# Retention heads 1 to 7 with seven block products for q with k and for value with gate

## The chip, the cores and the metric

The kernel is one program on one core of a Trainium2 chip. The metric is the device time of one execution in microseconds (us). The core's engines run side by side, each through its own queue of instructions in a fixed order: TensorE (PE in the profile, with PEld for its weight loads), VectorE (DVE), ScalarE (ACT), GpSimd (POOL) and SyncE (SP, which here issues DMA transfers). They wait for each other through semaphores.

## The reference, cut to what matters

The model has two layers over 512 latent tokens and 256 context tokens of width 1024, all in float32. Layer 0 is neighbourhood attention beside spatial gating, then a gated FFN with a short convolution. Layer 1 is a retention with eight heads, then an FFN of the same form. The change lies in the retention:

```python
def retention_mixer(h_ctx, h_lat, w_in, log_decay, gn_g, w_out, ctx_out):
    ...
    q, k, v, g = jnp.split(h_lat @ w_in, splits, axis=-1)   # 512 x 1024 times 1024 x 6144
    q = apply_rope(q.reshape(B, T, H, dk), cos, sin)        # H = 8, dk = 128, dv = 256
    k = apply_rope(k.reshape(B, T, H, dk) * dk ** -0.5, cos, sin)
    ...
    for d in range(2):                                      # forward and backward
        s_ctx = retention_final_state(rev(kc), rev(vc), lg)
        outs_lat.append(rev(retention_chunked(rev(q), rev(k), rev(v), lg, s_ctx)))
    # per-head norm of the sum, times silu(g), times w_out (2048 x 1024)
    y_lat = retention_output(outs_lat[0] + outs_lat[1], g, gn_g, w_out)
```

So for each head there are, of the latent tokens, a product for q and for k (1024 x 128 weights each), one for the value and one for the gate (1024 x 256 weights each), then scores, states and outputs of the head, and the head's share of the output projection, summed over heads into `y`.

## The kernel before, in words

**Split products.** A float32 product is made of three PE products in a faster format. `split` makes a high part with ACT (line 211) and the remainder with DVE (line 212); `mm3` then issues three matmuls (lines 256, 257, 258): high by high, high by low, low by high. Weights come from DRAM by SP into a raw buffer (`raw_unit`, three buffers), are split into a slot (`slot`; in the retention six slots `w0` to `w5`), and are named `rwk`, `rwq`, `rwv`, `rwg`, `rwo` here. `h0c` and `h1c` are the high and low parts of the normed tokens, which lie transposed in SBUF, the width along the partitions.

**A head of the retention** (`for h in range(8)`, line 1446): `proj_t` makes k (`rk`) and q (`rq`) of the latent tokens, 8 chunks of the contraction times 3 matmuls, each 128 x 512. `rope` takes them out of PSUM: two half copies by ACT (`swk`, `swq`, line 1259), a product by DVE (`m1k`, `m1q`, line 1260), a product by POOL (line 1261), a sum by DVE (line 1262), and a split. `nat` makes value and gate (`rn`), two token blocks at a time: 48 matmuls of 128 x 256 each for context value, latent value (two) and gate (two). Then scores (`rs`, `sd`), states (`stc`, `stl`), and the outputs within and across chunks (`ro`, `rx`), with the norm. `gated(h-1)` transposes the gated output of the head before (`rt`, then `gt`), and `out_group` multiplies it by two weight tiles: eight pieces `wr` of 128 x 512, six matmuls each, which DVE adds from PSUM to the four `y` tiles in SBUF (line 718; ACT copies for the first head, line 716). The pieces of a head are thus made during the next one; those of heads 6 and 7 are made at the end, in `out_last`. The `e` tiles are the head's decay weights, `acc` belongs to the adaLN products that are made in the background of the retention (`bg`).

**Seven products elsewhere.** Both FFNs already make their input products by blocks: of a 2 x 2 by 2 x 2 block product seven block products of sums are made instead of eight, with the weight sums on DVE, and context and latent outputs of FFN 0 are collected in DRAM by POOL (`yp`, four buffers, lines 1770 to 1774).

**Order.** The order of every engine's instructions is written out: `ORDER` is a packed table which `queue` decodes, and the instructions that the Python code makes are issued in its order. PSUM tiles come from three tags: A with four banks, B and C with two each.

## Time and profile before

| | |
|---|---|
| median of 3 runs | 1777.94 us (1776.95 to 1779.11) |
| profiled execution | 1775.4 us, of which the span of instructions is 1773.6 us |
| mean granted TensorE clock | 0.996 |
| busy: PE, DVE, ACT, POOL | 1747.3, 1394.7, 1025.0, 344.5 us |
| layer 0, attention and FFN | 0 to about 897 us |
| retention, heads 0 to 7 | about 897 to 1396 us |
| end of the retention and FFN 1 | 1396 to 1773.6 us |

The page gives busy time by engine, the span in 40 slices with busy tenths, the chain of work that ended last, the costliest groups of instructions, and the DMA transfers. Busy time of PE counts a matmul from its start to its modelled end, and matmuls overlap; how long one holds the array is read from the distance of starts in the timeline. The transposes `rt` of the head before mark where heads 1 to 7 begin: at about 949, 1015, 1081, 1146, 1212, 1277 and 1343 us.

### The profile page before, as it was taken

The page shows a single profiled execution, that of the slowest core. Times are in us where ns is not written, and L with a number is a line of the kernel's source. Part 1 is how long each engine was busy: PE and PEld are TensorE (multiplying, and loading weights), DVE is VectorE, ACT ScalarE, POOL GpSimd, SP SyncE. Part 2 cuts the span into 40 slices and gives each one's busy share as a digit, 9 for nine tenths or more (in the row PEclk, how much of TensorE's full clock was granted, in tenths as well). Part 3 has the DMA queues.
Part 4 walks back from the last instruction along what each step waited for, and adds up shares of the span by engine and source line. Part 5 has one row for each costly group of instructions (what it writes and reads, how often), then busy time and mean ns, then how long its engine had stood idle before and what let it go on. Part 6 is the DMA issues. An engine that isn't in the chain of part 4 may idle for free.

```text
span 1773.6 us, 28862 instructions
## 1 busy us (share of the span) xinstructions
PE 1747.3 (99%) x11024; PEld 1570.8 (89%) x11024; DVE 1394.7 (79%) x2363; ACT 1025.0 (58%) x1883; POOL 344.5 (19%) x462
## 2 busy tenths in 40 slices
PE   8999999999999999999999999999999999999997
PEld 4898888799999999999898998998999799999996
DVE  4887887898888878889877677666755799998896
ACT  7533667786556565656665434434444577767673
POOL 1102322230132321221311001101101200222212
PEclk9999999999999999999999999999999999999999
DMA  8345331364698877887643342341321335887763
GB/s 310 118 144 157 115 90 43 107 180 139 155 185 182 189 155 161 180 163 162 243 140 122 107 126 83 96 119 61 104 74 49 119 98 177 209 207 188 172 160 125
DMA packets 84398, 253.44 MB, mean 143 GB/s; under 512 B 11026, under 2 KB 11538, under 8 KB 84260
## 3 DMA queue, kind: packets, MB, share of 16 engines
q1 hardware_dynamic: 55044, 191.27, 34.2%
q0 software_dynamic: 26912, 51.95, 17.5%
q10 hardware_dynamic: 2304, 8.39, 1.2%
q8 instruction: 86, 1.41, 0.3%
q14 instruction: 52, 0.43, 0.1%
HBM read 191.80 MB, written 39.85 MB: 131 GB/s over the span
## 4 chain that ended last, share of the span: by engine, by line
PE 47%; DVE 1%; POOL 1%; ACT 1%; issue 0%; DVEq 0%; POOLq 0%; ACTq 0%
PE px L255 5%; PE rn L258 4%; PE rn L256 4%; PE rn L257 4%; PE wf L256 2%; PE wf L257 2%; PE wf L258 2%; PE py L255 2%; PE wr L258 1%; PE wr L257 1%; PE wr L256 1%; PE rk L257 1%; PE rk L256 1%; PE rk L258 1%; PE rq L258 1%; PE rq L257 1%
## 5 line engine op out<-in xcount | busy, mean ns | idle before, releaser
L366 DVE SCALAR_TENSOR_TENSOR acc<-ar,cs,acc 128x512 f32<-128x512 f32 x256 | 191.4, 768 | 7.3 <-DMA ar<-in_adaw 5.0
L255 PE MATMUL px<-hs,wc 128*128 128x384 f32 (+1 forms) x480 | 108.4, 308 | 0.2 <-ACT pre L1614 0.2
L1774 POOL DMA_DIRECT2D yf<-yp x64 | 55.5, 960 | 263.7 <-ACT yp L1770 236.7
L256 PE MATMUL rn<-rwv,h0c 128*128 128x256 f32 x384 | 106.6, 282 | 0.0
L258 PE MATMUL rn<-rwv,h1c 128*128 128x256 f32 x384 | 105.8, 281 | 0.4 <-DVE h1c L212 0.4
L257 PE MATMUL rn<-rwv,h0c 128*128 128x256 f32 x384 | 104.8, 280 | 0.0
L255 PE MATMUL px<-blk,wb 128*128 128x384 f32 (+1 forms) x480 | 103.3, 308 | 0.4 <-ACT pre L1614 0.4
L1770 ACT COPY yp<-wf 128x512 f32<-128x512 f32 x118 | 68.6, 583 | 51.6 <-PE wf L258 47.0
L1627 DVE SCALAR_TENSOR_TENSOR cv<-pre,cw,cv 128x769 f32<-128x769 f32 (+1 forms) x88 | 77.4, 884 | 22.5 <-ACT cv L1626 22.5
L1626 ACT ACTIVATE cv<-pre,cw 128x770 f32<-128x770 f32 (+1 forms) x88 | 80.9, 925 | 24.4 <-DVE pre L1619 22.1
L1614 ACT ACTIVATE pre<-px 128x256 f32<-128x256 f32 (+2 forms) x160 | 55.4, 370 | 54.1 <-PE px L255 32.5
L255 PEld LDWEIGHTS px<-hs,wc 128*128 128x128 f32 x480 | 80.8, 188 | 5.7 <-ACT pre L1614 0.5
L255 PEld LDWEIGHTS px<-blk,wb 128*128 128x128 f32 x480 | 79.2, 188 | 5.1 <-ACT pre L1614 1.0
L1630 DVE SCALAR_TENSOR_TENSOR cv<-pre,cw,cv 128x769 f32<-128x769 f32 (+1 forms) x88 | 77.5, 883 | 0.8
L258 PEld LDWEIGHTS rn<-rwv,h1c 128*128 128x128 f32 x384 | 71.7, 189 | 2.3 <-DVE h1c L212 0.7
L256 PEld LDWEIGHTS rn<-rwv,h0c 128*128 128x128 f32 x384 | 71.9, 188 | 2.1
L257 PEld LDWEIGHTS rn<-rwv,h0c 128*128 128x128 f32 x384 | 71.7, 189 | 1.5
L1774 POOL DMA_DIRECT2D yd<-yp x48 | 45.4, 973 | 135.2 <-ACT yp L1770 123.6
L257 PE MATMUL rn<-rwg,h0c 128*128 128x256 f32 x256 | 70.1, 280 | 0.0
L258 PE MATMUL rn<-rwg,h1c 128*128 128x256 f32 x256 | 69.9, 280 | 0.0
L255 PE MATMUL px<-hs,wd 128*128 128x384 f32 x240 | 69.9, 338 | 0.0
L256 PE MATMUL rn<-rwg,h0c 128*128 128x256 f32 x256 | 69.7, 279 | 0.0
(1546 smaller groups left out, 6398.9 us busy)
## 6 DMA issues: line engine op xcount, KB each, us to landing
ar<-in_adaw SPq DMA_DIRECT2D x96, 512.0 KB, 3.7
yf<-yp POOLq DMA_DIRECT2D x64, 256.0 KB, 4.9
yd<-yp POOLq DMA_DIRECT2D x54, 256.0 KB, 5.1
yd<-ypg POOLq DMA_DIRECT2D x54, 256.0 KB, 5.4
fin<-xd SPq DMA_DIRECT2D x8, 512.0 KB, 10.9
xn<-in_x SPq DMA_DIRECT2D x6, 512.0 KB
xb<-in_x SPq DMA_DIRECT2D x6, 512.0 KB
xd<-xb ACTq DMA_DIRECT2D x6, 512.0 KB, 3.6
```

The lines of the kernel that those rows point to most:

```text
L255: mm = lambda *p, **k: self.T.matmul(*p, skip_group_check=True, **k)
L256: mm(out, lhs[0], rhs[0], start=first, stop=False)
L257: mm(out, lhs[0], rhs[1], start=False, stop=False)
L258: mm(out, lhs[1], rhs[0], start=False, stop=last)
L366: V.scalar_tensor_tensor(out=acc[s], in0=raw[:, kk * 512 : kk * 512 + 512], scalar=self.cs[:, 8 * s + k : 8 * s + k + 1], in1=acc[s], op0= ...
L1614: S.activation(pre[:, i, c : c + w], ps[:, b : b + w], AF.Copy, scale=scale)
L1626: S.activation(d, s, AF.Identity, scale=w1, bias=b)
L1627: V.scalar_tensor_tensor(out=d[:, 1:W], in0=s[:, 0 : W - 1], scalar=w0, in1=d[:, 1:W], op0=ALU.mult, op1=ALU.add)
L1630: V.scalar_tensor_tensor(out=d[:, 0 : W - 1], in0=s[:, 1:W], scalar=w2, in1=d[:, 0 : W - 1], op0=ALU.mult, op1=ALU.add)
L1770: S.copy(v, ps)
L1774: G.dma_start((yd[t] if first else y[t])[:, o], v, accum_op=ALU.add)
```

## The change

For heads 1 to 7 the products of the latent tokens are made by blocks. Tokens (two halves of 256) and contraction (two halves of 512) make a 2 x 2 block matrix, `blk`; k with q, and value with gate, are the other two block columns. Seven products `X`, `Y`, `Z` are accumulated in three PSUM banks and read in between.

- `token_sums`, once at the end of head 0: four sums of the token blocks (`s1` to `s4`; `f` on POOL, then DVE, then splits). `s2` and `s4` lie in the space of the `y` tiles, `s3` over block 21 of the tokens.
- `k_unit`, `q_units`, `vg_units`: weight differences by `less` on POOL, in place in the raw buffers; four of 128 x 512 for q with k, four of 128 x 1024 for value with gate, each head. The results are split like the weights (`rwt1` to `rwt4`; halves of `rwq1` to `rwq3`). The raw weights of k and q and of the value's second half have two buffers of their own (`rawx`).
- `qk_lat`: seven products of 12 matmuls 128 x 256 (`xk`, `yk`, `zk`), summed in SBUF as `ks` and `qs` by ACT copies and DVE sums, on which `rope` then works. `vg_lat`: seven products of 24 matmuls 128 x 256 (`xv`, `yv`, `zv`). The context's value stays with `nat`.
- `out_away`: the pieces `wr` of heads 0 to 5 are copied by ACT into one of two `yp` buffers and sent by POOL to DRAM (`yd`), added there after the first head. In head 7 four loads on SP bring `y` back.
- Weight slots go from six to five.

Counts of instructions, before and after: PE matmuls 10882 and 10966 (1344 `rn` and 336 `rk`/`rq` fewer, 1764 of 128 x 256 more), DVE 2333 and 2400, ACT 1769 and 1915, POOL 467 and 579, SP 402 and 406.

```diff
-            rp = self.phase(ctx, "retp", 3, SLOT)
+            rp = self.phase(ctx, "retp", 2, SLOT)
...
-            order += [... ("w3", SLOT), ("w4", SLOT), ("w5", SLOT)]
+            order += [... ("w3", SLOT), ("w4", SLOT), ("rawx", 1024, 2), ("sx", 2048), ("yp", 512, 2)]
...
+            def less(out, x, y):
+                G.tensor_tensor(out=out, in0=x, in1=y, op=ALU.subtract)
...
+            def q_units(h):
...
+                w[11], w[21] = halves(d["wk"])
+                less(rk[:, H[0]], rq[:, H[0]], rk[:, H[0]])
+                less(rq[:, H[0]], rq[:, H[1]], rq[:, H[0]])
+                w["t", 1], w[22] = halves(self.slot(f"rwq1{h}"))
+                self.split(*w["t", 1], rk[:, H[0]])
+                self.split(*w[22], rq[:, H[1]])
...
+            def qk_lat(h, w):
...
+                qk_product(X, w[11], blk[11], "only")
+                S.copy(ks[:, A], X)
+                qk_product(Z, w[21], blk[12], "only")
+                V.tensor_tensor(out=ks[:, A], in0=ks[:, A], in1=Z, op=ALU.add)
+                qk_product(Y, w["t", 1], blk["s", 1], "only")
+                S.copy(qs[:, B], Y)
+                qk_product(X, w["t", 2], blk["s", 2], "onto")
+                S.copy(qs[:, A], X)
+                qk_product(X, w["t", 3], blk["s", 3], "onto")
+                V.tensor_tensor(out=qs[:, B], in0=qs[:, B], in1=X, op=ALU.add)
+                qk_product(Y, w[22], blk["s", 4], "onto")
+                V.tensor_tensor(out=qs[:, A], in0=qs[:, A], in1=Y, op=ALU.add)
+                qk_product(X, w["t", 4], blk[22], "onto")
+                S.copy(ks[:, B], X)
...
+            def vg_units(h):
...
+                v0, g0 = self.raw_unit(row(0, 0), f"rwv0{h}"), self.raw_unit(row(16, 0), f"rwg0{h}")
+                w[11] = parts(v0, "v0")
...
+                less(v0, g0, v0)
...
+                w["t", 1] = parts(v0, "t1")
+                less(g0, g1, g0)
...
+                w["t", 3] = parts(g0, "t3")
+                w[22] = parts(g1, "g1")
+                less(g1, g1, v0)
...
+            def out_away(f, w, first):
+                for t in toks:
+                    c = self.gcol(t)
+                    for n in range(2):
+                        ps = self.ps(f"wr{t}{n}", "B")
+                        for x, ((gh, gl), (wh, wl)) in enumerate(zip(f, w)):
+                            self.mm3(ps, (gh[:, c], gl[:, c]), (wh[:, H[n]], wl[:, H[n]]), x == 0, x == 1)
+                        z = rp.tile([P, 512], F32, name="ypr", tag="yp", bufs=2)
+                        S.copy(z, ps)
+                        if first:
+                            G.dma_start(yd[t][:, H[n]], z)
+                        else:
+                            G.dma_start(yd[t][:, H[n]], z, accum_op=ALU.add)
...
-                    psk = self.ps(f"rk{h}", "A")
-                    self.proj_t(psk, wk, 0)
-                    k_lat(h, psk)
-                    wq = qk(h, 0, "q")
-                    psq = self.ps(f"rq{h}", "A")
+                    w = q_units(h)
                     decay(h)
                     f = gated(h - 1)
-                    self.proj_t(psq, wq, 0)
-                    q_lat(h, psq)
+                    qk_lat(h, w)
                     self.bg()
                     if h < 7:
-                        self.out_group(f, w_out(h - 1), y, toks, h == 1, None, f"r{h - 1}")
+                        out_away(f, w_out(h - 1), h == 1)
...
+                    for t in toks:
+                        y[t] = self.ytile(t, f"yr{t}")
+                        self.load(y[t], yd[t])
```

The table `ORDER` is replaced as a whole (one line of it stands for all):

```diff
-c-pmlXLRJ)b>@8l3aJ1TfI{V*t4J1E%sDi3X0w}Qv%AR-(|M-jO!tHilQjyXFr#Eiqd2mHNA_wYTN+zFYiVuo`gqqX$79L)*p`pit6ke`uXoQ```CLgs>
+c-oD82ecdKb>{sCGlRi241mF)_woR|-g_^6y^@cQkL9sS6sy=oijpWxlqI>yawJ){<w%x`Y{|AP+p*)mPP}olC7Wz=a*{YcC)rKBn@#MT-JDH1C!1{c-h
...
```

What it moves, at three places in head 4. TensorE before, where q of head 4 ends and the first output piece of head 3 (`wr300`) begins; each row is a matmul, destination, then moving and stationary operand:

```order
L257 MATMUL rq4_11875<-h1c_8692,rwq4_11872 128x512
L258 MATMUL rq4_11875<-h0c_8691,rwq4_11872 128x512
L256 MATMUL rq4_11875<-h0c_8691,rwq4_11872 128x512
L256 MATMUL wr300_11947<-rwo30_11939,gt03_11882 128x512
L257 MATMUL wr300_11947<-rwo30_11939,gt03_11882 128x512
L258 MATMUL wr300_11947<-rwo30_11939,gt13_11883 128x512
L256 MATMUL wr300_11947<-rwo31_11944,gt03_11882 128x512
```

The same place after; the lines 269 to 271 are those of `mm3`, `rwq24` is a split weight difference and `s40r` a token sum:

```order
L269 MATMUL yk4_12132<-s41r_9692,rwq14_12092 128x256
L269 MATMUL xk4_12131<-h1c_8692,rwq24_12099 128x256
L269 MATMUL xk4_12131<-h0c_8691,rwq24_12099 128x256 x2
L269 MATMUL xk4_12131<-h1c_8692,rwq24_12099 128x256
L270 MATMUL wr00_12259<-rwo30_12251,gt03_12113 128x512
L269 MATMUL xk4_12131<-h0c_8691,rwq24_12099 128x256
L271 MATMUL wr00_12259<-rwo30_12251,gt03_12113 128x512
L269 MATMUL xk4_12131<-h0c_8691,rwq24_12099 128x256
```

The 512-wide projection is gone, and matmuls of several products and of the output piece alternate one by one.

GpSimd before, from the norm of head 3 to that of head 4 (`e`: decay weights, `swk` and `swq`: rope):

```order
L1407 TENSOR_TENSOR rrr3_11802<-rrr3_11802,mhalf_107 128x2
L1252 TENSOR_TENSOR e04_11876<-e04_11876,e14_11878 128x384
L1261 TENSOR_TENSOR swk4_11862<-swk4_11862,sin_9093 128x512
L1253 TENSOR_TENSOR e04_11876<-e04_11876,ident_95 128x128
L1261 TENSOR_TENSOR swq4_11925<-swq4_11925,sin_9093 128x512
L357 MEMSET acc180_12235 128x512
```

And after, from the first output piece on (`rwv04r` and so on are the raw weights of head 4):

```order
L1465 DMA yd0r_9101<-ypr_12266 128x512
L1489 TENSOR_TENSOR swk4_12227<-swk4_12227,sin_9095 128x512
L1465 DMA yd0r_9101<-ypr_12276 128x512
L1293 TENSOR_TENSOR rwv04r_12369<-rwg04r_12371,rwv04r_12369 128x1024
L1465 DMA yd1r_9102<-ypr_12286 128x512
L1489 TENSOR_TENSOR swq4_12237<-swq4_12237,sin_9095 128x512
L1465 DMA yd1r_9102<-ypr_12296 128x512
L1293 TENSOR_TENSOR rwg04r_12371<-rwg14r_12408,rwg04r_12371 128x1024
L1465 DMA yd2r_9103<-ypr_12306 128x512
L371 MEMSET acc180_12590 128x512
L1465 DMA yd2r_9103<-ypr_12316 128x512
L1477 TENSOR_TENSOR e04_12107<-e04_12107,e14_12109 128x384
```

Eight DMA issues and eight subtractions have come in between, and the rope's two products stand behind issues of output pieces.

ScalarE after, at the same place (before, it has the `gt` and `swq` of head 4 and the splits of `rwg40` here, and no copy of an output piece, as DVE added those):

```order
L1461 COPY ypr_12266<-wr00_12259 128x512
L1483 ACTIVATE swk4_12227<-ks4_12129 64x512 x2
L1461 COPY ypr_12276<-wr01_12269 128x512
L1483 ACTIVATE swq4_12237<-qs4_12130 64x512 x2
L225 ACTIVATE ah170_12357<-acc170_11622 128x512
L1461 COPY ypr_12286<-wr10_12279 128x512
L225 ACTIVATE rwt14_12437<-rwv04r_12369 128x1024
L225 ACTIVATE rk04_12225<-ks4_12129 128x512
L1461 COPY ypr_12296<-wr11_12289 128x512
L225 ACTIVATE rq04_12235<-qs4_12130 128x512
```

From the third on, each copy needs the buffer of the copy two before it, and the splits of weights and of the rotated k and q stand behind these copies.

More of the change, by code (lines that the diff above doesn't have):

```diff
@@ new lines, in q_units @@
+            def q_units(h):
+                d = hd[h]
+                rk = d["rk"]
+                rq = rawx(a["ret_qk"][h * P : (h + 1) * P], f"rwq{h}")
+                halves = lambda u: [[x[:, c] for x in u] for c in H]
+                w = {}
+                w[11], w[21] = halves(d["wk"])
[4 more added lines that the diff above has]
+                self.split(*w[22], rq[:, H[1]])
+                less(rq[:, H[1]], rq[:, H[1]], rk[:, H[0]])
+                less(rk[:, H[1]], rk[:, H[1]], rq[:, H[1]])
+                w["t", 2], w["t", 3] = halves(self.slot(f"rwq2{h}"))
+                self.split(*w["t", 2], rq[:, H[1]])
+                self.split(*w["t", 3], rq[:, H[0]])
+                w["t", 4] = halves(self.slot(f"rwq3{h}"))[0]
+                self.split(*w["t", 4], rk[:, H[1]])
+                return w
@@ L1423, in gated @@
                 if h == 7:
[L1424 removed]
+                    sx = rp.tile([P, 2, 2, 512], F32R, name="gt7", tag="sx", bufs=1)
+                    gt = [sx[:, i] for i in range(2)]
                 else:
```

415 lines of the change are left out of this document (285 added, 130 removed).

## The prediction

> **What bounds the kernel now.** I read the page's shares first, then the busy time by stage, then the chain and the waits of the retention, then TensorE's timeline. Shares and tenths of the span:
>
> ```profile
> PE 1747.3 (99%) x11024; PEld 1570.8 (89%) x11024; DVE 1394.7 (79%) x2363; ACT 1025.0 (58%) x1883; POOL 344.5 (19%) x462
> ...
> PE   8999999999999999999999999999999999999997
> ...
> DVE  4887887898888878889877677666755799998896
> ```
>
> TensorE (PE) is busy in every slice; the retention, 897 to 1396 us, lies in slices 21 to 32, where VectorE (DVE) is at its lowest. Because PE's busy time includes the pipeline, I take the stages apart. Columns: stretch, its length, then busy us and instructions of PE, PEld, DVE, ACT, POOL, then clock, DMA share, GB/s. The first row is head 0, the next two are heads 4 and 6, the last two are the seven-product FFNs of layers 0 and 1.
>
> ```profile
> 897.00:950.00 53.00, 53.00 (x426) 51.59 (x425) 38.85 (x69) 30.13 (x47) 6.20 (x8) 1.00 0.39 117
> 1146.35:1211.66 65.31, 65.31 (x453) 60.13 (x452) 41.81 (x75) 25.99 (x38) 5.57 (x8) 1.00 0.33 97
> 1277.64:1343.01 65.37, 64.89 (x449) 59.17 (x447) 40.13 (x69) 23.58 (x38) 6.89 (x9) 1.00 0.27 81
> 460.00:640.00 180.00, 180.00 (x936) 166.11 (x935) 148.79 (x211) 108.89 (x187) 50.40 (x65) 1.00 0.83 179
> 1440.00:1600.00 160.00, 159.24 (x1136) 147.96 (x1135) 153.60 (x241) 114.76 (x209) 26.74 (x32) 1.00 0.70 181
> ```
>
> A head takes 65.3 us and PE has no idle time in it, while DVE is at 64% and POOL (GpSimd) at 9%. So a head lasts as long as its matmuls take at their spacing, and fewer matmuls make it shorter, as long as nothing else becomes late. The FFN rows show that PE stayed full in this kernel beside a DVE at 83% (149 of 180) and nearly full at 96% (154 of 160).
>
> The spacing is read from starts, not from the mean length (a matmul's 0.39 or 0.28 us overlaps the next). Head 4, 14 starts of 128x512 and 27 starts of 128x256:
>
> ```profile
> 1148.21 0.39 PE L258 MATMUL rq<-h0c,rwq 128*128 128x512 f32 x1
> ...
> 1151.15 0.39 PE L256 MATMUL rq<-h0c,rwq 128*128 128x512 f32 x1
> ...
> 1158.60 0.28 PE L256 MATMUL rn<-rwv,h0c 128*128 128x256 f32 x1
> ...
> 1161.66 0.28 PE L258 MATMUL rn<-rwv,h1c 128*128 128x256 f32 x1
> ```
>
> 2.94/13 = 0.226 us for a 512-wide matmul, 3.06/26 = 0.1177 us for a 256-wide one.
>
> **The matmuls.** Per head the change removes 24 + 24 of `rk` and `rq` (512 wide: 48 x 0.226 = 10.9 us) and 192 of `rn` (22.6 us), and adds 84 of `xk`, `yk`, `zk` and 168 of `xv`, `yv`, `zv`, all 256 wide: 252 x 0.1177 = 29.7 us. That is -3.8 us a head, nearly all of it from value with gate: q with k falls only from 10.9 to 9.9 us, since seven products of half width replace six of their size. Seven heads: **-26.6 us**. The transposes, `wr`, `rkc`, scores and states stay.
>
> **The other engines.** Rows for the durations (group, count, busy us, mean ns):
>
> ```profile
> L718 DVE TENSOR_TENSOR yr<-wr,yr 128x512 f32<-128x512 f32 x40 | 27.4, 689 | 31.4 <-PE wr L258 31.1
> L1361 DVE TENSOR_TENSOR sd<-rs,e 128x256 f32<-128x256 f32 x24 | 9.5, 419 | 8.4 <-PE rs L258 8.3
> L212 DVE TENSOR_TENSOR rwg<-rwg31r,rwg 128x1024 fp32r<-128x1024 f32 x1 | 1.2, 1228 | 0.0
> L211 ACT ACTIVATE rwg<-rwg30r 128x1024 fp32r<-128x1024 f32 x1 | 1.1, 1067 | 0.0
> L1261 POOL TENSOR_TENSOR swk<-swk,sin 128x512 f32<-128x512 f32 x6 | 7.8, 1301 | 18.1 <-ACT swk L1259 18.1
> L1770 ACT COPY yp<-wf 128x512 f32<-128x512 f32 x118 | 68.6, 583 | 51.6 <-PE wf L258 47.0
> L1774 POOL DMA_DIRECT2D yd<-yp x48 | 45.4, 973 | 135.2 <-ACT yp L1770 123.6
> ```
>
> DVE, per head: three more 1024-wide weight splits (+3.7 us), five 512-wide ones for one 1024-wide (5 x 0.69 - 1.23 = +2.2), three 256-wide and three 512-wide sums out of PSUM (3 x 0.42 + 3 x 0.69 = +3.3), and the eight additions `yr<-wr` go (-5.5). So 41.8 becomes about 45.5 of a head of 61.5 us, 74%. ACT gets the same splits (about +5), four 256-wide and three 512-wide copies (about 3.2) and eight copies into `yp` (4.7): 26 becomes 39, 63%. POOL gets eight DMA issues (7.8 us) and eight subtractions: four 128x512 (5.2 us) and four 128x1024, which no row has; by the 512-wide row they take between 1.3 (no dearer) and 2.6 us (twice), and I take 2.4, near twice: 9.6. POOL goes from 6 to 28 us, 46%. None is full, so these cost nothing as sums. They can cost through lateness.
>
> **First price: DVE held by POOL.** In these rows a DVE operation with both inputs in SBUF runs long when a POOL operation is under way:
>
> ```profile
> 921.28 1.30 POOL L1261 TENSOR_TENSOR swq<-swq,sin 128x512 f32<-128x512 f32 x1 [0.89 <-ACT swq L1259]
> ...
> 921.89 1.23 DVE L212 TENSOR_TENSOR rk<-m1k,rk 128x512 fp32r<-128x512 f32 x1 [0.95 <-ACT rk L211]
> ...
> 1277.64 1.21 ACT gt L1432 x2
> 1280.01 0.69 DVE m1k L1260
> 1280.70 1.57 DVE acc L366
> 1282.30 0.83 DVE acc L366
> 1283.13 0.67 DVE gt L1433
> ...
> PE wr L258 <- DVE gt L1433: 0.5, 1, 0.5
> ```
>
> The split took 1.23 us where an operation of this size takes 0.69. The five rows after it are from the chain of head 6, where DVE lay behind schedule and PE's only wait of heads 2 to 7 followed, 0.5 us. The change adds 14.8 us of such POOL work a head, and some 31 of DVE's 45.5 us have, by the program's operands, two SBUF inputs (splits, masks, `acc`), so the hold is 0 to 14.8 us a head; I take 6, as a POOL operation holds the one DVE operation that meets it for part of its length. DVE then has 51.5 of 61.5 us, 84%, where FFN 0 had no idle PE. Late on DVE are the low halves of the weight splits and the sums `ks`, `qs`, behind which `swk`, `swq` and the scores wait. Bounds on PE: 0 (FFN 0) to 4 us a head (the whole gain); I take 0.7, near the 0.5 that such lateness cost once: **+5 us** for seven heads.
>
> The Trainium skill, SBUF — State Buffer, section Who interferes with whom, states that VectorE with two SBUF inputs and a reading GpSimd exclude each other for a whole instruction. The split of 1.23 us agrees. By the rule at its worst every added subtraction holds DVE throughout, which is the last rival below.
>
> **Second price: two `yp` buffers.** A piece of `wr` now goes PSUM, ACT copy (0.58), POOL issue (0.97), landing, before its buffer is free. The FFN's `yp` transfers are the nearest rows:
>
> ```profile
> yd<-yp POOLq DMA_DIRECT2D x54, 256.0 KB, 5.1
> ...
> DMA to landing us min/median/max: 2.3/5.0/9.0
> ...
>   DMA yf<-yp: 1.4, 1
> ```
>
> The last row says that `yp` made ACT wait once, 1.4 us in all; but there four buffers turn and here two. A turn is 0.6 + 1.0 + 2.3 to 9.0; with 4.5 us, a little under the median as DMA is at 0.33 here against 0.83, about 6 us, plus 2.4 where a subtraction stands ahead on POOL. PE's own order finishes the eight pieces over about 17.5 us (the spacings summed over the rows from `wr00` to `wr31`), and the eighth copy has three turns before it: 18 to 20 us. So ACT waits 1 to 3 us a head in the copy, and behind it on ACT stand splits (`rwg1`, `rwt3`, `rwt2`) whose weights PE takes some 5 us later. Bounds: 0 (landing 2.3) to 13 us a head (landing 9.0: 3 x 10.6 - 17.5 = 14, less some cover); I take 1, since PE has `zv` and `rn` to run meanwhile. Six heads send pieces away: **+6 us**.
>
> The Trainium skill, DMA: Bandwidth & Descriptors, fits a GpSimd-issued transfer with 2.0 us + bytes/436 KB per us, by which 256 KB would be 2.6 us and this term nothing; the sum would be 6 us lower. The trace's median of 5.0 decides.
>
> **Edits costed at little or nothing.** The token sums at the end of head 0 put eight sums on POOL (10.4 us) and some 16 operations (11 us) on DVE, which has 38.9 of 53.0 there: 50, or 94%, and POOL may hold some of it. The first product that needs them (`yk1`) comes after `xk1`. Bound 0 to 8; I take 1, since FFN 1 at 96% lost 0.8. The reuse of an accumulator (`xk` read, then added on) makes PE wait for a 0.4 us copy; other products stand between, 0 to 0.2 a head. One weight slot fewer: loads come later, DMA is at a third; 0 to 1 a head. The four loads of `y` on SP, 512 KB each, can start when head 7 has read its token sums, about 160 matmul rows (20 us) before the first `wrA` addition; the slowest such transfer is
>
> ```profile
> fin<-xd SPq DMA_DIRECT2D x8, 512.0 KB, 10.9
> ```
>
> so they are hidden.
>
> **Sum.** -26.6 + 5 + 6 + 1 = -14.6 us. Against the profiled execution's own 1775.4 us (span 1773.6) this gives 1760.8. The median of the runs, 1777.9, lies 2.5 us above that execution, and the next median is measured like it: 1763.3, **1763 us**.
>
> **Rivals.**
> - Full gain: PE stays full as in FFN 0. 1777.9 - 26.6 = 1751, and 1749 if the 1764 new products stand 1% closer (2 us). For it: the FFN rows, with the same kind of products. Against: those take their weight sums on DVE, not POOL, and have four `yp` buffers. Chance 0.27.
> - The buffers decide: landing about 6 us, 2.5 to 4 us lost a head for six heads, and the same 6 elsewhere: 1772 to 1781. For it: a maximum of 9.0. Against: little traffic here. 0.12.
> - The products aren't cheaper: 252 matmuls with other weights each take 0.130 us instead of 0.1177 (+3.1 us a head, 22 in all). Then 1773 with no stalls and about 1785 with all. Against: `rn` shows 0.1177 with alternating weights. 0.03.
> - Slower: POOL holds DVE until DVE is the bound. DVE's free time in the shorter head is 61.5 - 45.5 = 16 us; when holds and waits on POOL use 16 + 3.8 = 20 us a head, the gain is gone. Subtractions (14.8), if each holds throughout, and DMA issues (7.8), if they hold too, make 22.6: 68 us a head, 2.7 over the old one, 1777.9 + 19 = 1797. For it: each subtraction feeds a split that DVE and PE need in the same head. Against: in head 6 a hold cost PE 0.5 us, and FFN 1 ran at 96%. 0.13.
>
> **How the numbers follow.** The forecast as summed, 1754 to 1771: 0.45. About 0.2% (3.6 us) is what a measurement of this kernel can tell from no change: 1774.4 to 1781.5. Faster: 0.27 + 0.45 + half of the buffers' 0.12 = 0.78. Same: the other half of that, the dearer products and a piece of the last rival, 0.10. Slower: 0.12. The range leaves out the last rival and the far side of the first: 1749 to 1780.
>
> **What would show it.** Right: heads of 61 to 63.5 us, `xv` spaced 0.117, POOL near 28 us a head, DVE near 50, two-input DVE operations beside `rwg<-rwg,rwg` lengthened, ACT's copies into `yp` waiting for DMA by 1 to 3 us a head. Wrong: PE waiting for DVE splits by over 2 us a head, PE waiting for `yp` copies through `wr` and its PSUM banks, or 128x1024 subtractions well over 2.6 us, which would double the hold.

## The result, and the profile after

The changed kernel takes 1838.87 us (median of 4 runs, 1835.95 to 1839.49) against 1777.48 of the kernel before on the same chip: a ratio of 1.0341, interval 1.0323 to 1.0358. It is 61 us slower, where 15 us faster was forecast. The profiled execution took 1838.39 us, its span is 1836.6.

Shares of the span of the changed kernel, and the busy tenths of PE, DVE and POOL in 40 slices of 46 us:

```profile
PE 1754.9 (96%) x11108; PEld 1577.7 (86%) x11108; DVE 1504.3 (82%) x2430; ACT 1108.7 (60%) x2029; POOL 517.6 (28%) x574
...
PE   8999999999999999999989999889988989999998
...
DVE  4887878898788878888898787876867799998887
...
POOL 1102222311233222121354454444354110222221
```

PE has lost three points, and its tenths fall to 8 where POOL's rise to 4 and 5: in the retention. By stage, first of the kernel before, then of the changed one (head 0; heads 1 to 7, from the first transpose `rt` of head 0's output to that of head 7's; the rest. Columns as in the prediction: length, then busy us of PE, PEld, DVE, ACT, POOL, then clock):

```profile
896.00:948.52 52.52, 52.52 (x427) 51.32 (x426) 38.41 (x68) 30.49 (x48) 5.20 (x7) 1.00 0.39 120
948.52:1391.59 443.07, 442.59 (x3084) 408.38 (x3082) 283.25 (x496) 183.71 (x275) 50.64 (x64) 1.00 0.32 96
1391.59:1773.60 382.01, 367.15 (x2523) 337.22 (x2521) 340.03 (x535) 256.53 (x481) 75.65 (x93) 0.98 0.62 162
```

```profile
897.00:957.77 60.77, 53.92 (x429) 51.77 (x427) 51.72 (x80) 33.91 (x57) 22.04 (x17) 0.98 0.30 104
957.77:1454.19 496.42, 446.96 (x3180) 415.15 (x3180) 382.48 (x551) 263.06 (x414) 205.75 (x166) 0.97 0.42 109
1454.19:1836.60 382.41, 368.35 (x2517) 337.58 (x2515) 339.78 (x538) 257.84 (x481) 77.39 (x93) 0.98 0.64 168
```

Head 0 ends 9.2 us later, heads 1 to 7 take 53.4 us more, the rest is as it was (0.4). In heads 1 to 7 PE now stands idle for 496.4 - 447.0 = 49.5 us, where it had 0.5. DVE is busy in 77% of them. So it isn't full, and yet PE waits.

PE's waits there, the longest (what waits, for what: us in total, times, longest):

```profile
PE rt L1659 <- DVE rg L1646: 6.5, 3, 4.7
PE xv L269 <- DVE rwt L226: 5.9, 4, 1.9
PE yv L271 <- DVE rwt L226: 5.8, 3, 3.9
PE rx L270 <- ACT st L225: 5.7, 5, 2.1
```

They are spread over many consumers, most of them behind DVE. One place shows how it happens. The timeline of POOL and DVE in head 5, two subtractions `less`, and beside them the weight splits and one operation, `kd`, that takes an input from PSUM (columns: start, duration, both in us):

```profile
1280.39 2.73 POOL L1293 TENSOR_TENSOR rwg15r<-rwg15r,rwv05r 128x1024 f32<-128x1024 f32 x1 [3.31 <-issue]
1283.20 3.26 POOL L1293 TENSOR_TENSOR rwv15r<-rwv15r,rwg15r 128x1024 f32<-128x1024 f32 x1
```

```profile
1280.77 0.48 DVE L1523 SCALAR_TENSOR_TENSOR kd<-kn,e,kd 128x256 fp32r<-128x256 f32 x1
1281.19 3.02 DVE L226 TENSOR_TENSOR rwt<-rwg05r,rwt 128x1024 fp32r<-128x1024 f32 x1
1284.25 3.29 DVE L226 TENSOR_TENSOR rwt<-rwg15r,rwt 128x1024 fp32r<-128x1024 f32 x1
...
1289.06 1.21 DVE L226 TENSOR_TENSOR rwt<-rwv15r,rwt 128x1024 fp32r<-128x1024 f32 x1
```

A split of the same size takes 1.21 us with POOL quiet. The first one began 0.80 us into a subtraction and ended 1.09 us after that subtraction's end: it did its own 1.2 us almost wholly behind it. The next subtraction, 3.26 us long, shows the same from the other side. The wide subtraction itself takes 2.4 to 3.4 us, 2.75 on average, against 2.4 in the forecast. Added up over the records of heads 1 to 7, what DVE operations took beyond the short ones of their kind (same line, operation and shape; the mark is the kind's first tenth) was some 9 us before and is some 74 now: about 10 us a head.

`kd` began inside the first subtraction as well, and took its usual 0.48 us. That holds throughout: 37 DVE operations with both inputs in SBUF began inside one of the 56 subtractions, and all but one of them (it began 0.05 us before the subtraction's end) took longer than usual. The 30 with an input in PSUM that did so took no longer than elsewhere.

The dearest place is the start of head 7. DVE, POOL and PE:

```profile
1392.87 4.02 DVE L1638 TENSOR_SCALAR on<-of,rmv,rrr 128x256 f32<-128x256 f32 x1 [1.10 <-POOL rrr L1635]
...
1397.34 2.56 DVE L1646 TENSOR_TENSOR rg<-on,rg 128x256 f32<-128x256 f32 x1
```

```profile
1393.38 2.40 POOL L1293 TENSOR_TENSOR rwv07r<-rwg07r,rwv07r 128x1024 f32<-128x1024 f32 x1
1395.74 1.00 POOL L1477 TENSOR_TENSOR e<-e,e 128x384 f32<-128x384 f32 x1
...
1397.22 2.39 POOL L1293 TENSOR_TENSOR rwg07r<-rwg17r,rwg07r 128x1024 f32<-128x1024 f32 x1
```

```profile
1399.95 0.48 PE L1659 MATMUL rt<-ident,rg 128*128 128x128 f32 x1 [4.66 <-DVE rg L1646]
```

`on` is the group norm of head 6's output and takes 0.41 us as a rule; here it took 4.02, to the end of the decay product `e` (its record begins half a us ahead of the subtraction's; why it was held even so, the trace doesn't say), `rg` behind it 2.56 instead of 0.43, and the transpose that needs `rg` let PE wait 4.66 us. And it goes on: the windows before, in and after that wait have as their clock

```profile
1388.40:1395.00 6.60, 6.60 (x55) 6.55 (x56) 5.35 (x11) 4.48 (x8) 3.04 (x4) 1.00 0.02 3
1395.10:1399.90 4.80, 0.19 (x2) 0.00 (x0) 4.80 (x5) 1.33 (x2) 4.43 (x4) 0.87 0.00 0
1400.00:1405.40 5.40, 5.40 (x26) 5.40 (x27) 1.97 (x3) 0.69 (x1) 0.00 (x0) 0.50 0.00 0
1405.50:1411.00 5.50, 5.50 (x49) 5.50 (x48) 4.72 (x7) 4.02 (x6) 0.00 (x0) 1.00 0.00 1
```

After the wait PE ran at half clock for 5.4 us: 26 matmuls where the next 5.5 us have 49. So a wait of 4.7 us cost about 7.4. In heads 1 to 7 the mean clock is 0.97, which over 496 us is some 15 us of lost speed.

### The profile page after: what moved, and what is told of

It reads as the page before. It is cut to its first block, busy times and chain, and to the rows that moved or that the text cites. A ratio compares the mean times of both kernels' runs of the same rounds, so it can differ in the third digit from the quotient of the medians.

```text
span 1836.6 us, 29516 instructions
## 1 busy us (share of the span) xinstructions
PE 1754.9 (96%) x11108; PEld 1577.7 (86%) x11108; DVE 1504.3 (82%) x2430; ACT 1108.7 (60%) x2029; POOL 517.6 (28%) x574
## 5 line engine op out<-in xcount | busy, mean ns | idle before, releaser
L380 DVE SCALAR_TENSOR_TENSOR acc<-ar,cs,acc 128x512 f32<-128x512 f32 x256 | 196.4, 787 | 10.2 <-DMA acc<-in_adab_row 4.1
L269 PE MATMUL px<-blk,wb 128*128 128x384 f32 (+1 forms) x480 | 107.0, 308 | 0.0
L2002 ACT COPY yp<-wf 128x512 f32<-128x512 f32 x118 | 68.7, 584 | 60.5 <-PE wf L272 49.5
L2006 POOL DMA_DIRECT2D yd<-ypg x48 | 46.8, 1035 | 117.0 <-ACT ypg L2002 116.7
L269 PE MATMUL py<-blk,wc 128*128 128x384 f32 x240 | 68.7, 337 | 0.0
L225 ACT ACTIVATE wb<-s 128x512 fp32r<-128x512 f32 x80 | 49.1, 628 | 31.6 <-PE px L269 29.0
L225 ACT ACTIVATE wc<-q 128x512 fp32r<-128x512 f32 x80 | 48.9, 625 | 22.3 <-PE py L269 11.0
L226 DVE TENSOR_TENSOR wb<-s,wb 128x512 fp32r<-128x512 f32 x80 | 54.3, 686 | 9.2 <-ACT wb L225 8.9
L226 DVE TENSOR_TENSOR wc<-q,wc 128x512 fp32r<-128x512 f32 x80 | 54.2, 687 | 4.2 <-ACT wc L225 3.9
L270 PE MATMUL wf<-fo,g 128*128 128x512 f32 x144 | 56.3, 397 | 0.4 <-ACT yp L2002 0.4
L271 PE MATMUL wf<-fo,g 128*128 128x512 f32 x144 | 56.4, 395 | 0.1
L272 PE MATMUL wf<-fo,g 128*128 128x512 f32 x144 | 55.5, 394 | 0.0
```

The lines of the kernel that those rows point to most:

```text
L225: self.S.activation(hi, src, AF.Copy)
L226: self.V.tensor_tensor(out=lo, in0=src, in1=hi.bitcast(F32), op=ALU.subtract)
L269: mm = lambda *p, **k: self.T.matmul(*p, skip_group_check=True, **k)
L270: mm(out, lhs[0], rhs[0], start=first, stop=False)
L271: mm(out, lhs[0], rhs[1], start=False, stop=False)
L272: mm(out, lhs[1], rhs[0], start=False, stop=last)
```

## The experiments

Throughout, "subtractions" are the 56 operations `less` on GpSimd. Times are medians; the kernel before had 1775.6 to 1776.9 us in these series.

**1. The subtractions on two columns** (`e1_tiny_subs`).

```diff
-                G.tensor_tensor(out=out, in0=x, in1=y, op=ALU.subtract)
+                G.tensor_tensor(out=out[:, :2], in0=x[:, :2], in1=y[:, :2], op=ALU.subtract)
```

> The 56 weight subtractions on GpSimd work on 2 of their columns (so the weight differences are not made); everything else, the seven products, splits, copies and sends, is as in the changed kernel. Theory L (GpSimd's subtractions hold VectorE's operations with two SBUF inputs; 70 us of hold in heads 1 to 7, and TensorE waits for the late splits): some 60 us of the 61 us loss are gone and part of the gain appears, 1765 to 1785 us, VectorE's weight splits back at 1.22 us. Theory D (the pieces sent away through two buffers and the send issues cost the time): 1830 us or more. Theory P (seven products with their extra splits and sums can't be fed in this order): 1820 us or more.

Measured: 1783.46 us, ratio 1.0043 (1.0028 to 1.0058), in the range of theory L. 55 of the 61 us are gone with the length of these 56 instructions; all else of the change is in place. Heads 1 to 7:

```profile
955.29:1398.82 443.53, 429.91 (x3180) 402.49 (x3181) 328.98 (x551) 262.75 (x414) 116.41 (x166) 1.00 0.47 122
```

PE's idle time falls from 49.5 to 13.6 us, and the clock is 1.00.

**2. Two memsets in place of each subtraction** (`e2_memset_subs`): GpSimd stays busy, and whoever needs the sum waits for it, but nothing is read.

```diff
-                G.tensor_tensor(out=out, in0=x, in1=y, op=ALU.subtract)
+                G.memset(out, 0.0117)
...
+                G.memset(out, 0.0213)
...
```

> Each of the 56 subtractions on GpSimd is replaced by two memsets of the same tile (the differences are not made): GpSimd is busy for about as long at the same place (2 x about 1.1 us for 128x1024, 2 x 0.55 for 128x512), the splits wait for it as before, but GpSimd reads nothing. Theory L: near the run with 2 columns, within 10 us of it, and VectorE's splits at 1.22 us. Rival Q (the subtraction is one more step in line between load and split, and its place in GpSimd's queue makes the splits late): near the changed kernel, 1820 to 1840 us.

Measured: 1786.78 us, ratio 1.0061 (1.0044 to 1.0078). GpSimd's queue and the place of the sums in it cost 3 us, its reading 52. The memsets keep GpSimd busy for less time, though: 87 us, where the subtractions take 119.

**3. Sixteen of 512 columns of each added piece sent to DRAM** (`e3_small_pieces`).

```diff
-                            G.dma_start(yd[t][:, H[n]], z, accum_op=ALU.add)
+                            G.dma_start(yd[t][:, 512 * n : 512 * n + 16], z[:, :16], accum_op=ALU.add)
```

> The 40 adding sends of output pieces (heads 1 to 5) carry 16 of 512 columns; issues, copies and order stay. Theory L: no change against the changed kernel, 1830 to 1842 us. Theory D, as far as landing and traffic go: 1800 us or less. What is left after this run for D are the issues on GpSimd.

Measured: 1837.78 us, ratio 1.0346 (1.0331 to 1.0361), as the changed kernel. The landing of the pieces is no part of the loss.

**4. The kernel before with as many subtractions beside it** (`e4_before_plus_subs`): 28 of 128x512 and 28 of 128x1024 on a tile of their own, which nothing waits for; three wide ones in a row behind each `rope` of q, four narrow ones and a wide one behind each norm.

```diff
+                for w in widths:
+                    G.tensor_tensor(out=dum[:, :w], in0=dum[:, :w], in1=dum[:, 1024 : 1024 + w], op=ALU.subtract)
```

> The kernel before, with 28 subtractions of 128x512 and 28 of 128x1024 on GpSimd added in the retention, on a tile that nothing else uses (after the second rope product and after the norm of each head). No data depend on them. Theory L in its plain form (hold becomes TensorE's waiting one for one): some 30 to 70 us slower than before, 1810 to 1845 us. If VectorE's 36% of free time in a head of the kernel before takes up the hold: under 10 us slower; then the loss of the change needs both the hold and VectorE's added work. Rivals D and P: no more than 2 us slower.

Measured: 1830.87 us, ratio 1.0308 (1.0293 to 1.0324). Without any of the products changed, about as much reading (109 us of subtractions) costs 55 us, as theory L has it in its plain form. DVE's free time did not take up the hold. Heads 1 to 7 of that run:

```profile
948.90:1449.40 500.50, 463.61 (x3084) 422.35 (x3082) 342.68 (x496) 184.48 (x275) 163.42 (x121) 0.96 0.28 85
```

DVE is busy in 68% of them, and PE is idle for 37 us and at a clock of 0.96. So DVE need not be near full.

**5. The control to it, memsets instead** (`e8_before_plus_memsets`): in the loop above, two `G.memset(dum[:, :w], v)` for each subtraction. (Experiment 4 and this control also take a smaller DMA scratch area than the kernel before.)

> Control for the run that added 56 subtractions to the kernel before (1831): two memsets of the same tile in the place of each, so GpSimd is about as long busy at the same places and reads nothing. Theory L: within 4 us of before. If GpSimd's being busy is the cause, or writes contend as reads do: 1800 us or more.

Measured: 1787.23 us, ratio 1.006 (1.0045 to 1.0075). GpSimd kept busy costs 11 us, where theory L had at most 4, but far less than the other forecast; its reading costs 44 more. The memsets take 83 us, the subtractions took 109; what that difference is worth isn't known, but at the price of the memsets it would be 3 us.

The Trainium skill, SBUF — State Buffer, section Who interferes with whom, says that a VectorE instruction with two SBUF inputs contends with a GpSimd instruction that reads SBUF, and not with one that only writes. Experiments 2 and 5, against the changed kernel and experiment 4, agree: 52 and 44 us hang on the reading.

**6. The subtractions on VectorE** (`e5_subs_on_vector`), each put into VectorE's queue a few places behind the last reader of what it overwrites.

```diff
-                G.tensor_tensor(out=out, in0=x, in1=y, op=ALU.subtract)
+                eng = V if w[0][0] in "vgqk" else G
+                eng.tensor_tensor(out=out, in0=x, in1=y, op=ALU.subtract)
...
```

> The changed kernel with its 56 weight subtractions on VectorE instead of GpSimd, each placed in VectorE's order between the split that last reads the old content and the split that needs the result; all else as in the changed kernel, nothing left out. VectorE gets 4 x 0.69 + 4 x 1.22 = 7.6 us more work a head. Theory L: the hold of the subtractions is gone, so it is near the run with 2 columns (1783) plus what 7.6 us more a head on VectorE cost; 1780 to 1800 us, clearly under the changed kernel. Rival (VectorE's sum of work is what counts, held or not): 7.6 us a head of work in place of 10 us of hold, so 1820 us or more.

Measured: 1836.09 us, ratio 1.0333 (1.0318 to 1.0349). Theory L missed, and the number is the one that the rival gave. But the run doesn't show that the rival's cause is at work, as the waits of DVE tell:

```profile
DVE rwv02r L1295 <- DMA rwg02r<-in_ret_vg: 5.3, 1, 5.3
DVE rwg03r L1295 <- DMA rwg13r<-in_ret_vg: 4.6, 1, 4.6
```

At the places chosen the weights had not landed, and DVE stood with its whole queue behind it, 25 us in all. In heads 4 and 5, with 1.7 us of that, a head took 67.9 and 66.4 us, against 74.6 and 71.0 in the changed kernel and 63.8 and 63.0 in experiment 1. A later place wasn't tried, so what the subtractions would cost on DVE stays open.

**7. No reading on GpSimd in the retention** (`e6_no_pool_reads`): the subtractions and the products of `rope` and `decay` on two columns, the token sums as memsets.

```diff
-                G.tensor_tensor(out=sw, in0=sw, in1=sin, op=ALU.mult)
+                G.tensor_tensor(out=sw[:, :2], in0=sw[:, :2], in1=sin[:, :2], op=ALU.mult)
...
-                        G.tensor_tensor(out=t, in0=x[0][:, c].bitcast(F32), in1=x[1][:, c].bitcast(F32), op=ALU.add)
+                        G.memset(t, 0.0117)
```

> The changed kernel with GpSimd reading nearly nothing in the retention: subtractions, rope products and decay products on 2 columns, token sums as memsets (differences, rope, decay products and token sums are thus not made). It shows what is left of the loss without any hold. If the remaining hold (rope, decay, token sums: some 20 us of GpSimd work per head and head 0's 13 us) explains why the run with 2 columns is at 1783 instead of 1751: 1755 to 1765 us. If the seven-product form has another cost of its own (splits, sums and copies that come late, more steps between product and use): 1772 us or more.

Measured: 1771.65 us, ratio 0.9973 (0.9964 to 0.9983): what the change gives where nothing is held is 4.7 us, not 26.6. So the seven-product form has a cost of its own, as the second forecast had it (the value lies 0.35 us below its bound). The "20 us per head" of the first is too much: the `rope` and decay products take some 5 us a head in the changed kernel. Heads 1 to 7:

```profile
949.62:1386.66 437.04, 427.55 (x3180) 401.37 (x3180) 315.78 (x551) 262.31 (x414) 93.49 (x166) 1.00 0.48 124
```

**8. The kernel before with the same products left out** (`e7_before_no_pool_reads`; `sw` and the decay products on two columns).

> The kernel before with rope and decay products on GpSimd on 2 columns (not made otherwise). The hold in its heads was 8.5 us in all and TensorE had no idle time: within 3 us of before. If it is 10 us or more faster, the hold cost TensorE more than the waits show.

Measured: 1776.09 us, ratio 0.9997 (0.9988 to 1.0007). The few reads that the kernel before had cost it nothing.

**9 and 10. Only one size of the subtractions on two columns** (`e9_tiny_1024`, `e10_tiny_512`): the edit of the first experiment where the width is 1024, or 512.

> The changed kernel with the 28 wide subtractions of value and gate (128x1024) on 2 columns; the 28 of q and k (128x512) stay whole. The wide ones carry about 80 of the 117 us of GpSimd subtraction. Theory L (each reading subtraction excludes VectorE operations with two SBUF inputs, and VectorE's lateness passes on to TensorE in proportion): two thirds of the 55 us go, 1796 to 1808. Rival P (position: only the subtractions that feed the next product at once cost, and those of q and k stand directly ahead of qk's products): less than half goes, over 1812.

> The reverse: the 28 subtractions of q and k on 2 columns, the wide ones whole. Theory L: one third of the 55 us goes, 1816 to 1828. Rival P: more than half goes, under 1812.

Measured: 1798.76 us (ratio 1.0131, 1.0115 to 1.0146) and 1825.47 us (1.0282, 1.0266 to 1.0297). Both lie in the ranges of theory L. The wide ones carry 40 us, the narrow ones 13, together 53 of 55: the more GpSimd reads, the more is lost. It isn't quite in proportion: 40 for 77 us of wide subtractions, 13 for 42 us of narrow ones.

**11. The token sums as memsets** (`e11_memset_token_sums`), one line of experiment 7 alone.

> The changed kernel with the eight GpSimd additions of the token sums, at the end of head 0, as memsets of the same tiles (VectorE's part of the token sums stays). Head 0 lost 9 us in the change. If GpSimd's reading holds VectorE there (94% busy by the prediction's count): 4 to 8 us less, 1831 to 1835. If it is VectorE's own added work of 11 us: within 2 us of the changed kernel, 1837 to 1840.

Measured: 1831.23 us (1.031, 1.0295 to 1.0326), 7.6 us less than the changed kernel; in the traces head 0 ends 5.2 us earlier. Of the 9.2 us that head 0 lost, most is again the reading, by eight instructions.

**12. No reading, and small pieces** (`e12_no_reads_tiny_pieces`): experiment 7 with `S.copy(z[:, :16], ps[:, :16])` and 16 columns sent, for the added groups.

> The kernel without GpSimd reads, and beside that only 16 of 512 columns of each added output piece are copied by ScalarE and sent (those of the second to sixth group; the first group stays whole). If ScalarE's copies, or the wait for their landing, keep that kernel 20 us above the full gain: 1755 to 1764. If what is left is the order of the matmuls and their own spacing: within 3 us of 1771.7.

Measured: 1769.91 us (0.9968, 0.9958 to 0.9977). That is 1.7 us under experiment 7, within the spread of the two: copies and pieces hold back some 2 us, if any.

**13 and 14. VectorE relieved of the weights' low halves** (`e13_narrow_lows` in the changed kernel, `e14_no_reads_narrow_lows` in that of experiment 7).

```diff
+    def narrow(self, hi, lo, src):
+        self.S.activation(hi, src, AF.Copy)
+        n = (slice(None),) * (len(lo.shape) - 1) + (slice(0, 16),)
+        self.V.tensor_tensor(out=lo[n], in0=src[n], in1=hi.bitcast(F32)[n], op=ALU.subtract)
...
-                self.split(u[0], u[1], d["rk"])
+                self.narrow(u[0], u[1], d["rk"])
...
+                w = [w[0], w[0]]
...
```

> The changed kernel with all GpSimd subtractions whole, but VectorE makes the low halves of the weights of heads 1 to 7 (seven splits a head) on 16 columns only, and TensorE reads the high half in their place, in as many matmuls. This takes about 12 us a head of VectorE's own work away, those rwt splits that were held longest (21.9 us of 70 over the seven heads), and TensorE's waits for them. Theory L (the loss is VectorE's lateness, work plus holds, passed on): with some 14 us a head less to do VectorE is no longer late, and over two thirds of the 55 us come back: 1778 to 1800. Rival (GpSimd's own lateness, by its 104 us of subtractions and what they wait for, sets the end; VectorE is only held): 1815 to 1839, since GpSimd's work and its place stay.

> The same relief of VectorE in the kernel without GpSimd reads (1771.7), which stays 20 us above the full gain. If what is left there is VectorE's lateness (its weight splits): 1755 to 1764. If it is the order and the spacing of the matmuls themselves (switching between accumulators, the pieces of head 7 and the tail): 1767 to 1772.

Measured: 1805.83 us (1.0161, 1.0146 to 1.0176) and 1770.3 us (0.9964, 0.995 to 0.9978). Neither theory of the first had it: half of the loss came back, and 35 us of reading remain, the difference of the two runs. The trace says why the relief did so little. A split of 16 columns, in head 5, and POOL beside it:

```profile
1239.05 4.79 DVE L231 TENSOR_TENSOR rwt<-rwv05r,rwt 128x16 fp32r<-128x16 f32 x1 [0.68 <-ACT rwt L229]
```

```profile
1238.96 1.62 POOL L1496 TENSOR_TENSOR swk<-swk,sin 128x512 f32<-128x512 f32 x1
1240.18 1.24 POOL L1472 DMA_DIRECT2D yd1r<-ypr  x1
1240.79 3.01 POOL L1298 TENSOR_TENSOR rwg05r<-rwg15r,rwg05r 128x1024 f32<-128x1024 f32 x1
```

The small split took 4.79 us and ended with the subtraction. A hold has POOL's length, whatever the size of what is held; the excess over the seven heads is some 68 us, hardly under 74. Yet it costs half as much, so the loss isn't set by the sum of the holds alone; how much of a hold reaches PE depends on the work around it. The second answers what was left of experiment 7: VectorE's splits are not it.

**15 to 18. The subtractions in pieces** (`e15_chop256`, `e16_chop128`: of 256 or 128 columns, issued one directly behind the other; `e17_chop256_all`: token sums, `rope` and decay products too; `e18_chop256_on`: as 15, and `on` as another form of instruction).

```diff
-                G.tensor_tensor(out=out, in0=x, in1=y, op=ALU.subtract)
+                self.chopped(out, x, y, ALU.subtract)
...
+        w, n = (out.shape[1], 1 if len(out.shape) == 3 else 256)
+        for c in range(0, w, n):
+            d = slice(c, min(w, c + n))
+            self.G.tensor_tensor(out=out[:, d], in0=x[:, d], in1=y[:, d], op=op)
...
```

> The changed kernel, the same sums, but each GpSimd subtraction is issued in pieces of 256 columns (four for 1024, two for 512), one directly behind the other. GpSimd reads as many numbers in the same places. Theory H (a hold lasts as long as the one GpSimd instruction that is under way; short VectorE operations of the group norm and the decay, needed by TensorE at once, were held 2.5 to 4 us, TensorE then waited 5 us and ran at half clock for 5 us more): a hold now ends after about 0.7 us, the long waits and the half clock go, and over half of the 55 us comes back: 1785 to 1812. Rival C (VectorE's capacity: it loses the whole time in which GpSimd reads, however cut): 1830 to 1845.

> The same in pieces of 128 columns (eight and four). Theory H: holds of about 0.45 us; as good as the pieces of 256 or better by up to 10 us, unless GpSimd's own time, which grows from 104 to about 140 us over the seven heads, makes its sums late: 1780 to 1812. Rival C: 1835 to 1860, since GpSimd reads for longer.

> Pieces of 256 columns for the subtractions, the additions of the token sums, the products of the rotary embedding and of the decay: all that GpSimd reads in the retention, in all eight heads. Theory H: 3 to 8 us less than with the subtractions alone in pieces, since head 0 lost 7 us by the token sums. Rival C: the same as with the subtractions alone, within 3 us.

> The kernel with the subtractions in pieces of 256 columns; beside that the 28 group norm operations `on<-of,rmv,rrr`, each a TENSOR_SCALAR, are the same arithmetic as SCALAR_TENSOR_TENSOR with the factor `rrr` read as a stretched second input. In the trace of the pieces one TENSOR_SCALAR of head 7 took 4.43 us, the whole length of four pieces and a decay product, while two-input operations beside pieces took 0.5 us more only; TensorE waited 3.5 us for it and then ran at half clock for 5.5 us (2.7 us lost). Theory S (a TENSOR_SCALAR gets in only when GpSimd stops reading, a two-input operation between any two pieces): the hold of 4 us goes, head 7 falls from 63.2 to 56 or 58 us, the time by 5 to 8 us: 1828 to 1832. Rival (any VectorE operation that starts second waits for the whole run of pieces): head 7 stays at 62 to 64, 1835 to 1839.

Measured: 1836.71, 1834.81, 1839.01 and 1836.18 us (ratios 1.0342, 1.0336, 1.0356 and 1.0341, intervals of 0.0016 to 0.0023 to either side). Theory H fell: no piece helps. Rival C gave the times of the first and the third; the second came out just under its range. Heads 1 to 7 in pieces of 128:

```profile
957.88:1448.97 491.09, 445.04 (x3180) 409.97 (x3180) 352.28 (x551) 263.45 (x415) 274.30 (x434) 0.98 0.43 110
```

Its mechanism doesn't fit, though: DVE's excess did fall, to some 55 us with pieces of 256 and 42 with 128. But POOL's busy time rose from 206 to 240 and 274 us, and ACT, which splits the sums, waited for them 30 and 52 us instead of 16. PE's idle time stayed near 50 us (44 and 46), with less of it behind DVE (36 us whole, 21 and 15 in pieces) and more behind ACT (14, then 22 and 30). The operation `on` of head 7 was held through all four pieces of 256 and the decay product behind them (first line, experiment 15), and as SCALAR_TENSOR_TENSOR just as long (second line, experiment 18, where theory S missed):

```profile
1389.96 4.43 DVE L1639 TENSOR_SCALAR on<-of,rmv,rrr 128x256 f32<-128x256 f32 x1 [1.10 <-POOL rrr L1636]
```

```profile
1391.63 4.55 DVE L1639 SCALAR_TENSOR_TENSOR on<-of,rmv,rrr 128x256 f32<-128x256 f32 x1 [1.09 <-POOL rrr L1636]
```

Other operations beside pieces took only some 0.5 us longer (`rg` 0.94 instead of 0.43). What lets the one in between two pieces and not the other is open.

## Why the prediction was wrong

The step that failed is "First price: DVE held by POOL", and in it the way from a hold to PE. The hold itself was taken as 6 us a head with bounds of 0 to 14.8, and measured 10. But of this PE was to lose 0.7 a head, at most 4; it lost 55 us over seven heads by experiment 1, 7.9 a head. The term of +5 was +52 to +55.

Three things in that step went astray:

- It took the FFNs, where PE is full or nearly so beside a DVE at 83% and 96%, as the measure of what lateness costs. GpSimd's groups of these stages, before the change, were not looked at. In FFN 1 (1440 to 1600 us):

```profile
L1774 POOL DMA_DIRECT2D yf<-yp x29 | 25.1, 932 | 149.1 <-ACT yp L1770 149.0
...
L357 POOL MEMSET acc<- 128x512 f32 x1 | 0.5, 524 | 1.4 <-DVE al L212 1.4
```

Issues of transfers and a memset, and no arithmetic: GpSimd read nothing there that could hold DVE. It is the same in the stretch of FFN 0 (460 to 640 us), from which the lower bound of 0 came: issues and four memsets. A busy DVE is not a held one. Experiment 4 shows the loss with DVE at 68%, experiment 13 with DVE relieved.
- It priced lateness by one case, 0.5 us, behind a POOL operation of 1.3 us. The eight new ones of a head take 1.3 to 3.4 us, and each feeds splits that PE needs in the same head.
- It bounded the loss by the gain. Nothing bounds it so; PE's waits bring a lower clock with them, which the step did not have at all. Against experiment 7 PE is busy for 447.0 instead of 427.6 us with the same matmuls: 19 us, of which the mean clock of 0.97 explains some 15.

The other terms, each by its own measure:

| term | forecast | measured |
|---|---|---|
| matmuls | -26.6 | -15.0: PE busy in heads 1 to 7, 442.6 before, 427.6 in experiment 7, at clock 1.00 in both |
| hold, heads 1 to 7 | +5 | +52 to +55 (experiments 1, 2) |
| two `yp` buffers | +6 | about 2 or less (experiments 3, 12) |
| token sums | +1 | +9.2 in head 0, of which 5 to 8 by reading (experiment 11) |
| not in the sum | 0 | +9.5: PE idle in heads 1 to 7 of experiment 7, where nothing is held; mostly behind ACT (`rx` 4.1, `ac` 2.5) |

In the traces of before and after the sum closes so: heads 1 to 7, -15.0 for the matmuls, +49.0 of idle time, +19.4 of longer busy time; head 0 +9.2; the rest +0.4: 63.0, the difference of the spans.

**Matmuls.** The term was mis-sized. The 256-wide products of value with gate stand 0.118 us apart in experiment 7, as forecast, but the 336 starts of `xk` are 0.127 us apart on average and the 168 of `yk` 0.13, instead of 0.1177: 6 us by themselves over the 581 records of q with k. Matmuls of other products grew too (`ro`, `wr`, `rx`, `stl`: 4 us), and six more `wrA` fall into head 7 (2 us). That the products aren't cheaper was a rival at 0.130 for all; for those of q with k alone it came near. Why those are further apart, the runs don't settle; the order table makes PE change its accumulator more often there (some 920 changes from a 256-wide matmul in heads 2 to 6, against 310 before).

**Second price.** It hardly occurred. The pieces land as quickly as estimated, and ACT waited for them 2.1 us in all:

```profile
  DMA yd0r<-ypr: 1.8, 2
  DMA yd1r<-ypr: 0.3, 1
...
DMA to landing us min/median/max: 2.4/4.1/6.8
```

**Token sums.** The count of DVE was right, about 50 us in head 0 (51.7 of 60.8). That this is covered was not, for the same reason as above: 9.2 us lie beyond the bound of 8.

**The rivals.** The last one named the right engines: GpSimd's subtractions hold VectorE, the time goes beyond the old one. Its condition was wrong: it needed holds and waits of 20 us a head, so that DVE has no free time; holds of 10 us a head were enough for a loss of 61 us in all, and 1797 was too little. The chance of slower, 0.12, went by that condition.

Of the signs named beforehand, "128x1024 subtractions well over 2.6 us" and two-input operations lengthened were there (2.75 us on average, up to 3.4; a split of 3.02 for 1.21). PE's wait for DVE splits stayed under the 2 us a head that was named (11.7 us for `xv` and `yv`); it was spread over `rt`, `rx`, `rs`, `kn`, `ac` as well.

## What to carry to other kernels

GpSimd arithmetic that reads SBUF is not a free helper beside a VectorE on whose short operations TensorE waits: here 56 subtractions, 109 to 119 us of GpSimd time (in the changed kernel 28 of 2.75 us and 28 of 1.49 us on average), cost 44 to 55 us, the more the longer they read, with VectorE busy in 68% or 77% of the time. Memsets of the same tiles on the same engine cost only 3 to 11 us. So before such work is put there, look at which VectorE operations with both inputs in SBUF will run beside it, and at how soon after each its consumer starts; busy shares tell little. That advice is drawn from the traces, and no run tested it by another order. And a price taken from the rows of another stage holds only if the engine in question does the same kind of work there.

## What the runs showed of the hardware

- In the changed kernel GpSimd's reading held the VectorE operations with both inputs in SBUF (36 of 37 that began inside a subtraction), and none of the 30 with an input in PSUM. The group norm operation `on`, which takes one tile and two columns of factors from SBUF, was held too (all 9 that began inside a subtraction in experiment 4). A held operation lasts as long as GpSimd goes on: 128x16 took 4.79 us, 128x256 took 4.02 to 4.55 instead of 0.41, through several GpSimd instructions in a row. Cutting a GpSimd instruction into pieces moved the loss from VectorE to GpSimd (206 to 274 us busy) and left the time nearly as it was (1834.81 to 1839.01 against 1838.87 us).
- TensorE ran at half clock after a short wait: 0.50 for 5.4 us after a wait of 4.7 us. A shorter one did it as well. The windows around a wait of 2.15 us in head 2 (before, in it, after it, back again; the half clock began some 1.3 us after the wait's end):

```profile
1085.00:1087.80 2.80, 2.80 (x26) 2.80 (x25) 2.80 (x3) 1.12 (x2) 2.72 (x4) 1.00 0.27 111
1088.00:1090.10 2.10, 0.04 (x1) 0.00 (x0) 2.04 (x4) 1.69 (x4) 0.50 (x1) 1.00 0.76 96
...
1091.10:1094.70 3.60, 3.60 (x15) 3.02 (x14) 2.53 (x7) 0.04 (x1) 0.00 (x0) 0.55 1.07 309
1094.80:1098.00 3.20, 3.20 (x24) 3.02 (x23) 2.56 (x9) 1.20 (x3) 0.91 (x2) 0.98 0.37 150
```

The Trainium skill, TensorE: Matmul & The Clock Gate, part 1, says that the clock falls to half after an idle window of about 3.4 us, and comes back after as long a busy one. The half clock and its length agree (the trace's clock records in heads 1 to 7 have stretches of 3.4 and 6.8 us); that a wait of 2.15 us was enough does not follow from an idle window of that length, and here the measurement decides. Not every wait of that size did it: after one of 2.50 us in experiment 7 the clock was 1.00.
